# Inverting the softmax row sums of paired attention heads by two 32x32 block turns around a short reciprocal

## The chip, the cores and the metric

The kernel runs on one core of a Trainium2 chip. The metric is device time in microseconds (us). One core has a matrix engine (PE), which loads weights (PEld) and runs matmuls into PSUM; a vector engine (DVE); a scalar engine with activation functions (ACT); a general engine (POOL); and SyncE (SP), which here issues the DMAs. Each engine works through its own list of instructions in a fixed order, and engines wait for each other through semaphores.

## The reference, cut to what matters

The program is a transformer block with three branches (forgetting attention, a diagonal state-space branch called S5, attention to a memory), followed by two layers of a second kind (grouped-query attention, dilated attention, a feed-forward part). Sequence length is 512, model width 1024, and everything is float32. What the change touches is the division by the softmax sum:

```
s = q k^T (+ bias, mask);  p = softmax(s);  out = p v
```

which the kernel computes as `out = (exp(s - m) v) * (1 / sum(exp(s - m)))`. It is done for the 12 heads of the forgetting attention, and in each of the two layers for 8 heads of the grouped-query and 4 heads of the dilated attention.

## The kernel before, in words

All matmuls that feed a result of full precision are done in three passes. A float32 operand is split into a high part (`wh`, `h`, `ph`) and a low part (`wl`, `l`, `pl`). For weights, `split` casts the strip `wr`, which a DMA brought, to `wh` on ACT (L93), and subtracts on DVE or, for every few strips, on POOL (L96) to get `wl`. For activations `hsplit` does the same with ACT (L229) and DVE (L237). `pmm` is the PSUM tile of a projection; its three passes are L124 (`wh` by `h`), L125 (`wh` by `l`) and L126 (`wl` by `h`).

Attention is written as a `unit` of heads. For each head and each key block, L327 computes scores into PSUM (`ps`), ACT takes the exponential `pe` (L395) and casts it to `ph` (L397), DVE subtracts to `pl` (L399), and three matmuls (L416 to L418) add the block into `ppv`. The value operand is widened by 64 columns of ones, so that 64 of the 128 rows of `ppv` hold the head's output and the other 64 rows all hold the same row of 512 softmax sums. There is one `ppv` buffer in PSUM: the next head cannot start before this one is copied out.

`out_item(j)` does that after the head's last matmul. Two ACT copies take the sums to half of the rows of `rs` (L443) and the outputs to half of the rows of `y` (L444; in the first block it is called `yf`). After each second head of a pair, L446 inverts `rs` as a whole (128x512) on DVE and POOL multiplies (L447). There are 18 pairs: six in the first block, and in each layer four of the grouped-query attention and two of the dilated one. In the text, the six pairs of a layer are called pair 1 to pair 6, in the order of time.

What sets the order in which an engine works is neither written out by hand nor in a table:

```
with tile.TileContext(nc, schedule_with_timeline_sim=True) as tc:
```

The tile framework plays the program through a timeline of its own and fixes each engine's list from it, when the kernel is built. A change of what one operation is takes part in that, and can move instructions of all engines. One schedule-only dependency (no wait on the chip) keeps each weight cast behind the matmul that was written last before it:

```
ins = self.nc.scalar.copy(h[:, 0:m], r[:, c:c + m])
if self.pe is not None:
    self.tc.add_manual_dep(ins.ins, self.pe, self.AFTER, reason="weights")
eng.tensor_tensor(out=l[:, 0:m], in0=r[:, c:c + m], in1=f32(h)[:, 0:m], op=ALU.subtract)
```

Tiles of 128x512 come from one ring of 73 buffers (`self.u`).

Of the kernel before, what the change touches and what calls it, by code (L numbers as in the profile page):

```python
# [9 lines left out]
F32 = mybir.dt.float32  # L10
# [231 lines left out]
class Att(Core):  # L242
# [44 lines left out]
    def rows(self, mc, tag, psum_tag, out=None):  # L287
# [7 lines left out]
            nc.scalar.copy(out[96:128], pt[96:128])  # L295
        return out

    def unit(self, nh, sregs, tregs, qk, vsl, dst, extra=None, nq=4, hd=64, orow=None, fold=None):


# [3 lines left out]
        nc = self.nc  # L304
# [99 lines left out]
        def pv_item(j, i):  # L404
            ph, pl, pvs = st.pop(("p", j, i))
            pv = st["pv", j]
            mm = nc.tensor.matmul
            for x, (g, kb, c) in enumerate(pvs):
                vh, vl = vsl(j, g, kb)
                o = c  # L410
                f = i == 0 and x == 0
                z = i == nt - 1 and x == len(pvs) - 1
                if not isinstance(c, slice):
                    o = slice(0, 4 * (c[1] - c[0]))
                h, lo = self.like(ph[:, o], c), self.like(pl[:, o], c)
                mm(self.cut(pv, c), vh, h, start=f, stop=False)  # L416
                mm(self.cut(pv, c), vl, h, start=False, stop=False)  # L417
                mm(self.cut(pv, c), vh, lo, start=False, stop=z)  # L418
            if i == nt - 1:
                out_item(j)  # L420

        def vrow(j):

            if own_sum:
                return slice(0, 128)
            o = 64 * (j % 2) if orow is None else orow(j)
            return slice(o, o + 64)

        def out_item(j):
            pv = st.pop(("pv", j))  # L430
            v = vrow(j)
            if own_sum:
                rb = self.u(name="rb")
                pb = self.p("m")
                nc.tensor.matmul(pb, self.selr1[j], st["mr"], start=True, stop=True)
                nc.scalar.copy(rb, pb)
                nc.vector.tensor_tensor(out=dst(j), in0=pv, in1=rb, op=ALU.mult)
                return
            if j % 2 == 0:
                st["rs"] = self.u(name="rs")  # L440
            rows = slice(64 * (j % 2), 64 * (j % 2) + 64)
            rs, y = st["rs"], dst(j)
            nc.scalar.copy(rs[rows], pv[64 - v.start:128 - v.start])  # L443
            nc.scalar.copy(y[rows], pv[v])  # L444
            if j % 2 == 1:
                nc.vector.reciprocal(out=rs, in_=rs)  # L446
                nc.gpsimd.tensor_tensor(out=y, in0=y, in1=rs, op=ALU.mult)  # L447

        s = [(lambda j=j, q=q: s_item(j, q)) for j in range(nh) for q in range(nq)]
# [1671 lines left out]
```

## Time and profile before

| | before |
|---|---|
| median of 3 runs (lowest, highest) | 2417.26 us (2416.67, 2422.07) |
| the profiled execution: its time | 2420.52 us |
| its span in the profile | 2418.5 us |
| mean granted TensorE clock | 0.984 |
| PE busy, share of the span | 2310.7 us, 96% |
| DVE busy | 1508.5 us, 62% |
| ACT busy | 1055.8 us, 44% |
| POOL busy | 875.4 us, 36% |

Busy time counts an engine's instructions, and the end of a matmul is modelled, so PE at 96% still has gaps. About 2 us of the execution's time lie outside its span.

### The profile page before, as it was taken

What the parts mean: (1) busy time and instruction counts of PE and PEld (TensorE: products, weight loads), DVE (VectorE), ACT (ScalarE), POOL (GpSimd) and SP (SyncE); (2) the same over time, 40 slices, a digit from 0 to 9 for tenths busy, and PEclk for the clock granted to TensorE, in tenths of its full rate; (3) what the DMA queues carried; (4) which work ended last, traced back from release to release, by engine and by line L of the source; (5) the groups of instructions that cost most, each with busy time, mean ns of one, the idle gap of its engine ahead of it and who ended that gap; (6) DMA issues with size and microseconds to landing.
All of it is one profiled execution on the core that took longest, in us unless ns stands there. A gap on an engine that the chain in (4) does not pass through costs nothing.

```text
span 2418.5 us, 32948 instructions
## 1 busy us (share of the span) xinstructions
PE 2310.7 (96%) x12071; PEld 1933.5 (80%) x12098; DVE 1508.5 (62%) x2467; ACT 1055.8 (44%) x1973; POOL 875.4 (36%) x722
## 2 busy tenths in 40 slices
PE   6999999998999899999999999999899999999999
PEld 5877777877788877788888888888778888888888
DVE  6666778666899788657378673257864746422222
ACT  4354553453333436653444324334565433523432
POOL 2443556733232284235132223126521713222212
PEclk9999999999999999999999999999999999999999
DMA  5211122313576331122247563242211314223322
GB/s 171 78 44 53 44 84 95 118 49 115 207 258 247 117 107 52 53 83 85 68 132 260 199 219 122 79 140 75 79 44 51 116 53 140 75 94 111 100 84 87
DMA packets 105617, 265.37 MB, mean 110 GB/s; under 512 B 13664, under 2 KB 23408, under 8 KB 105456
## 3 DMA queue, kind: packets, MB, share of 16 engines
q1 hardware_dynamic: 104304, 261.50, 32.2%
q8 instruction: 95, 1.56, 0.3%
q10 hardware_dynamic: 1152, 1.77, 0.2%
q14 instruction: 66, 0.54, 0.1%
HBM read 244.72 MB, written 9.44 MB: 105 GB/s over the span
## 4 chain that ended last, share of the span: by engine, by line
PE 75%; DVE 11%; issue 5%; POOL 4%; ACT 3%; DMA 2%; SPq 0%; ACTq 0%; another core or an unknown queue 0%; POOLq 0%; DVEq 0%
PE pmm L124 19%; PE pmm L126 19%; PE pmm L125 19%; PE ps L327 5%; PE ppv L416 1%; PE ppv L418 1%; PE pmm L141 1%; PE ppv L417 1%; PE pmm L142 1%; PE pmm L140 1%; DVE wl L96 1%; DVE l L239 1%; ACT wh L93 1%; POOL wl L96 1%; DVE adacc L521 1%
## 5 line engine op out<-in xcount | busy, mean ns | idle before, releaser
L96 POOL TENSOR_TENSOR wl<-wr,wh 128x512 fp32r<-128x512 f32 x346 | 489.6, 1434 | 1160.3 <-ACT wh L93 1037.2
L126 PE MATMUL pmm<-h,wl 128*128 128x512 f32 (+1 forms) x2104 | 823.4, 392 | 9.0 <-POOL wl L96 5.3
L124 PE MATMUL pmm<-h,wh 128*128 128x512 f32 (+1 forms) x2104 | 823.3, 392 | 7.2 <-ACT wh L93 4.3
L125 PE MATMUL pmm<-l,wh 128*128 128x512 f32 (+1 forms) x2104 | 819.7, 390 | 0.0
L126 PEld LDWEIGHTS pmm<-h,wl 128*128 128x128 f32 x2104 | 399.6, 190 | 94.3 <-POOL wl L96 7.7
L124 PEld LDWEIGHTS pmm<-h,wh 128*128 128x128 f32 x2104 | 399.8, 190 | 86.2 <-ACT wh L93 5.6
L125 PEld LDWEIGHTS pmm<-l,wh 128*128 128x128 f32 x2104 | 399.6, 190 | 78.4 <-DVE l L237 0.8
L93 ACT CAST wh<-wr 128x512 fp32r<-128x512 f32 (+1 forms) x692 | 387.5, 612 | 146.3 <-DMA wr<-in_w 85.9
L96 DVE TENSOR_TENSOR wl<-wr,wh 128x512 fp32r<-128x512 f32 x346 | 276.2, 827 | 39.3 <-ACT wh L93 34.6
L399 DVE TENSOR_TENSOR pl<-pe,ph 128x512 fp32r<-128x512 f32 (+4 forms) x168 | 113.6, 689 | 132.1 <-ACT ph L397 131.1
L237 DVE TENSOR_TENSOR l<-r,h 128x512 fp32r<-128x512 f32 x64 | 46.6, 728 | 221.3 <-ACT h L229 216.5
L1010 DVE SCALAR_TENSOR_TENSOR x<-pmm,ada,x 128x512 f32<-128x512 f32 (+1 forms) x88 | 60.0, 682 | 178.7 <-PE pmm L126 178.3
L521 DVE SCALAR_TENSOR_TENSOR adacc<-adw,cact,adacc 128x512 f32<-128x512 f32 x168 | 154.4, 921 | 4.1 <-DMA adw<-in_wada 0.9
L327 PE MATMUL ps<-qk,qk 128*128 128x512 f32 (+4 forms) x416 | 140.8, 366 | 12.6 <-DVE unm L352 8.6
L1033 ACT ACTIVATE r<-pmm 128x512 f32<-128x512 f32 x62 | 37.1, 598 | 246.0 <-PE pmm L126 246.0
L395 ACT ACTIVATE pe<-ps 128x512 f32<-128x512 f32 (+4 forms) x168 | 84.5, 503 | 114.7 <-PE ps L327 113.3
L327 PEld LDWEIGHTS ps<-qk,qk 128*128 128x128 f32 x416 | 79.3, 192 | 29.4 <-DVE unm L352 12.4
L124 PE MATMUL pmm<-yh,wh 128*128 128x512 f32 (+1 forms) x244 | 90.4, 374 | 5.8 <-ACT yh L1466 3.8
L125 PE MATMUL pmm<-yl,wh 128*128 128x512 f32 (+1 forms) x244 | 90.4, 371 | 2.7 <-DVE yl L1128 2.7
L397 ACT CAST ph<-pe 128x512 fp32r<-128x512 f32 (+4 forms) x168 | 89.1, 530 | 6.5 <-ACT pe L395 0.4
L126 PE MATMUL pmm<-yh,wl 128*128 128x512 f32 (+1 forms) x244 | 89.5, 369 | 0.0
L352 DVE TENSOR_REDUCE unm<-ps 128x1 f32<-128x512 f32 (+2 forms) x112 | 65.1, 597 | 25.6 <-PE ps L327 25.3
(393 smaller groups left out, 3925.0 us busy)
## 6 DMA issues: line engine op xcount, KB each, us to landing
wr<-in_w SPq DMA_DIRECT2D x324, 512.0 KB
adw<-in_wada SPq DMA_DIRECT2D x192, 256.0 KB
xs<-xg SPq DMA_DIRECT2D x136, 64.0 KB
wr<-in_w SPq DMA_DIRECT2D x22, 384.0 KB
xd<-x SPq DMA_DIRECT2D x16, 256.0 KB
x<-xd SPq DMA_DIRECT2D x16, 256.0 KB
x<-in_x SPq DMA_DIRECT2D x16, 128.0 KB
x<-in_x SPq DMA_DIRECT2D x8, 256.0 KB
```

The costliest lines, as they stand in the source:

```text
L93: ins = self.nc.scalar.copy(h[:, 0:m], r[:, c:c + m])
L96: eng.tensor_tensor(out=l[:, 0:m], in0=r[:, c:c + m], in1=f32(h)[:, 0:m], op=ALU.subtract)
L124: mm(out, wh, ah, start=start, stop=False)
L125: mm(out, wh, al, start=False, stop=False)
L126: self.pe = mm(out, wl, ah, start=False, stop=stop).ins.name
L327: mm(outs[i] if len(r.shape) == 2 else outs[i].rearrange("p (r i) -> p r i", r=r.shape[1]), w, r, start=first and i == 0, stop=last and i ...
L352: nc.vector.tensor_reduce(out=nm, in_=pts[0], axis=AX.X, op=ALU.max, negate=True)
L395: nc.scalar.activation(out=e[:, w], in_=pt[:, w], func=AF.Exp)
L397: nc.scalar.copy(ph[:, w], e[:, w])
L399: nc.vector.tensor_tensor(out=pl[:, w], in0=e[:, w], in1=f32(ph)[:, w], op=ALU.subtract)
L521: nc.vector.scalar_tensor_tensor(out=acc, in0=w, scalar=cc, in1=acc, op0=ALU.mult, op1=ALU.add)
L1010: nc.vector.scalar_tensor_tensor(out=x[j][:, s], in0=pm[:, s], scalar=ada[:, c + j:c + j + 1], in1=x[j][:, s], op0=ALU.mult, op1=ALU.add)
```

## The change

`out_item` no longer inverts the whole of `rs`. A new function turns `rs` by 32x32 blocks into a tile `rt` (each block of 32 rows and 32 columns is transposed in its place). Since all 32 rows of a block hold the same 32 sums, column 0 of a turned block holds these sums, one in each row. The reciprocal is taken of that column of each of the 16 blocks in a row (128x16, a stride of 32), into `ri`. The second turn reads `ri` with each column repeated 32 times and writes the inverted sums over `rs`. The rest of `out_item` stays. `rt` takes one more tile of the ring, for a short time. All lines behind the new function stand ten lines further down (L443 becomes L453, and so on).

```diff
+    def inv_rows(self, rs):
+
+
+        nc = self.nc
+        rt = self.u(name="rt")
+        nc.vector.transpose(out=rt, in_=rs)
+        ri = self.t(self.base, [128, 16], F32, "ri", 2)
+        nc.vector.reciprocal(out=ri, in_=rt.rearrange("p (b c) -> p b c", c=32)[:, :, 0])
+        nc.vector.transpose(out=rs.rearrange("p (b c) -> p b c", c=32), in_=ri.unsqueeze(2).to_broadcast([128, 16, 32]))
...
             if j % 2 == 1:
-                nc.vector.reciprocal(out=rs, in_=rs)
+                self.inv_rows(rs)
                 nc.gpsimd.tensor_tensor(out=y, in0=y, in1=rs, op=ALU.mult)
```

**Pair 4 of the first layer.** This is ACT's list in the stretch at the end of the grouped-query attention: the exponentials of the last key block, the weight casts `wh` of a strip of the next projection, the splits `h` of the four pair outputs `y` for the branch projection, and the two copies of the pair's second head (`rs`, `y`). Before:

```order
L397 CAST ph_10071<-pe_10069 128x512
L93 CAST wh_10085<-wr_9823 128x512
L93 CAST wh_10089<-wr_9823 128x512
L945 ACTIVATE g_10120<-pmm_10095 128x512
L229 CAST h_10122<-y_9064 128x512
L229 CAST h_10126<-y_9441 128x512
L229 CAST h_10130<-y_9717 128x512
L443 COPY rs_9988<-ppv_9975 64x512
L444 COPY y_9989<-ppv_9975 64x512
L229 CAST h_10134<-y_9989 128x512
```

The same place after the change:

```order
L407 CAST ph_10107<-pe_10105 128x512
L453 COPY rs_10024<-ppv_10011 64x512
L454 COPY y_10025<-ppv_10011 64x512
L93 CAST wh_10125<-wr_9855 128x512
L93 CAST wh_10129<-wr_9855 128x512
L955 ACTIVATE g_10160<-pmm_10135 128x512
L229 CAST h_10162<-y_9088 128x512
L229 CAST h_10166<-y_9469 128x512
L229 CAST h_10170<-y_9749 128x512
L229 CAST h_10174<-y_10025 128x512
```

The two copies, which wait for the head's last matmul, now stand ahead of two weight casts, one gate activation and three splits, instead of behind them. On PE the same place reads, after the change, with the pair's last value matmul in the second of these rows and the branch projection behind it:

```order
L427 MATMUL ppv_10011<-ph_10107,vl_15_91 128x512
L428 MATMUL ppv_10011<-pl_10109,vh_14_90 128x512
L124 MATMUL pmm_10188<-h_10162,wh_10041 128x512
L124 MATMUL pmm_10300<-h_10162,wh_10041 128x512
L124 MATMUL pmm_10415<-h_10162,wh_10125 128x512
```

As before the change, the first matmul behind the pair's last one reads the split of pair 1 (`h_10162`); before, that split stood ahead of the copies on ACT, and now it stands behind them. The second layer has the same move.

**Pair 2 of the first layer.** ACT's list at the end of pair 2, where a strip's casts `wh` are followed by four casts of rotated queries and keys (`qk`). Before:

```order
L93 CAST wh_9487<-wr_9081 128x512
L93 CAST wh_9491<-wr_9081 128x512
L691 CAST qk_9525<-xg_8893 64x512
L691 CAST qk_9528<-xg_8893 64x512
L691 CAST qk_9534<-xg_9011 64x512
L443 COPY rs_9440<-ppv_9427 64x512
L444 COPY y_9441<-ppv_9427 64x512
```

After:

```order
L453 COPY rs_9468<-ppv_9455 64x512
L454 COPY y_9469<-ppv_9455 64x512
L93 CAST wh_9519<-wr_9105 128x512
L93 CAST wh_9523<-wr_9105 128x512
L701 CAST qk_9557<-xg_8917 64x512
L701 CAST qk_9560<-xg_8917 64x512
L701 CAST qk_9566<-xg_9035 64x512
```

And PE behind the pair's last value matmul, after the change:

```order
L428 MATMUL ppv_9455<-pl_9503,vh_14_90 128x512
L337 MATMUL ps_9655<-qk_9281,qk_9272 128x128
L124 MATMUL pmm_9685<-h_7648,wh_9519 128x512
L125 MATMUL pmm_9685<-l_7656,wh_9519 128x512
L126 MATMUL pmm_9685<-h_7648,wl_9520 128x512
```

The copies moved ahead of the strip's casts, and the projection that uses this strip (`wh_9519`, and `wl_9520`, which POOL makes) follows the pair's last matmul on PE at once; before, two of its matmuls stood ahead of that matmul.

**Pair 5 of the first layer.** DVE's list from the inversion to `qv`, the first step of a chain of small operations on which PE waits later. Before:

```order
L446 RECIPROCAL rs_10309<-rs_10309 128x512
L653 TENSOR_TENSOR xs_10488<-xs_10488,rope_7979 128x512
L96 TENSOR_TENSOR wl_10583<-wr_10460,wh_10582 128x512
L664 TENSOR_TENSOR xg_10487<-xg_10487,xs_10488 128x512
L951 SCALAR_TENSOR_TENSOR g_9850<-g_9850,pmm_10557 128x512
L96 TENSOR_TENSOR wl_10587<-wr_10460,wh_10586 128x512
L653 TENSOR_TENSOR xs_10539<-xs_10539,rope_7979 128x512
L660 TENSOR_SCALAR qv_10577<-ps_10531 128x4x2 x2
```

After:

```order
L303 STREAM_TRANSPOSE rt_10476<-rs_10349 128x512
L305 RECIPROCAL ri_10478<-rt_10476 128x16
L306 STREAM_TRANSPOSE rs_10349<-ri_10478 128x512
L96 TENSOR_TENSOR wl_10541<-wr_10186,wh_10540 128x512
L96 TENSOR_TENSOR wl_10545<-wr_10186,wh_10544 128x512
L663 TENSOR_TENSOR xs_10532<-xs_10532,rope_8003 128x512
L961 SCALAR_TENSOR_TENSOR g_9882<-g_9882,pmm_10601 128x512
L96 TENSOR_TENSOR wl_10627<-wr_10504,wh_10626 128x512
L96 TENSOR_TENSOR wl_10631<-wr_10504,wh_10630 128x512
L674 TENSOR_TENSOR xg_10531<-xg_10531,xs_10532 128x512
L663 TENSOR_TENSOR xs_10583<-xs_10583,rope_8003 128x512
L670 TENSOR_SCALAR qv_10621<-ps_10575 128x4x2 x2
```

The inversion moved ahead of two subtractions `wl` that stood before it, so that two more operations lie between it and `qv`.

## Rows read from the trace of the kernel before

**Rows 1.** The page's busy time of PE and DVE (us, share of the span, instructions), and its chain of work that ended last, by engine.

```profile
PE 2310.7 (96%) x12071; PEld 1933.5 (80%) x12098; DVE 1508.5 (62%) x2467; ACT 1055.8 (44%) x1973; POOL 875.4 (36%) x722
...
PE 75%; DVE 11%; issue 5%; POOL 4%; ACT 3%; DMA 2%; SPq 0%; ACTq 0%; another core or an unknown queue 0%; POOLq 0%; DVEq 0%
```

**Rows 2.** The groups of DVE instructions by line and shape: busy us, mean ns of one, idle time before them and what ended it. The inversion, and the DVE operations nearest to those that are new.

```profile
L446 DVE RECIPROCAL rs<-rs 128x512 f32<-128x512 f32 x18 | 60.2, 3344 | 18.7 <-ACT rs L443 18.7
...
L237 DVE TENSOR_TENSOR l<-r,h 128x512 fp32r<-128x512 f32 x64 | 46.6, 728 | 221.3 <-ACT h L229 216.5 <-issue 4.2
...
L653 DVE TENSOR_TENSOR xs<-xs,rope 128x512 f32<-128x512 f32 x34 | 32.2, 946 | 25.4 <-DMA xs<-xg 25.2
...
L1122 DVE TENSOR_SCALAR rd<-ph 128x512 f32<-128x512 f32 x12 | 7.1, 593 | 2.1 <-POOL ph L1284 1.6 <-POOL ph L1280 0.3
...
L375 DVE RECIPROCAL uri<-usm 128x16 f32<-128x16 f32 x2 | 0.5, 253 | 1.6 <-ACT jk L349 1.6
```

**Rows 3.** POOL's waits: total us, times, longest us.

```profile
POOL y L447 <- DVE rs L446: 34.1, 7, 11.3
```

**Rows 4.** The timeline of ACT at the end of pair 4 of the first layer: start us, us, engine line operation tiles, in brackets the idle time before and what ended it.

```profile
1030.90 1.14 ACT L93 CAST wh<-wr 128x512 fp32r<-128x512 f32 x2
1031.95 0.59 ACT L945 ACTIVATE g<-pmm 128x512 f32<-128x512 f32 x1
1032.44 1.64 ACT L229 CAST h<-y 128x512 fp32r<-128x512 f32 x3
1035.82 0.58 ACT L443 COPY rs<-ppv 64x512 f32<-64x512 f32 x1 [1.73 <-PE ppv L418]
1036.42 0.58 ACT L444 COPY y<-ppv 64x512 f32<-64x512 f32 x1
1041.25 0.63 ACT L229 CAST h<-y 128x512 fp32r<-128x512 f32 x1 [4.25 <-POOL y L447]
```

**Rows 5.** The timeline of PE at the same place: the pair's last value matmul, and the first matmuls of the branch projection.

```profile
1035.39 0.39 PE L418 MATMUL ppv<-pl,vh 128*128 128x512 f32 x1
...
1035.78 0.94 PE L124 MATMUL pmm<-h,wh 128*128 128x512 f32 x3
1036.56 0.39 PE L125 MATMUL pmm<-l,wh 128*128 128x512 f32 x1
```

**Rows 6.** The timeline of ACT at the same place of the second layer.

```profile
1836.15 1.65 ACT L229 CAST h<-y 128x512 fp32r<-128x512 f32 x3
1839.47 0.58 ACT L443 COPY rs<-ppv 64x512 f32<-64x512 f32 x1 [1.67 <-PE ppv L418]
```

**Rows 7.** The timeline of ACT at the end of pair 2 of the first layer.

```profile
972.21 1.14 ACT L93 CAST wh<-wr 128x512 fp32r<-128x512 f32 x2
973.26 1.90 ACT L691 CAST qk<-xg 64x512 fp32r<-64x512 f32 x3
975.18 0.58 ACT L443 COPY rs<-ppv 64x512 f32<-64x512 f32 x1
```

**Rows 8.** The timeline of PE there: two matmuls of the projection and the pair's last value matmul, and the gap that comes nine us later.

```profile
973.72 0.58 PE L124 MATMUL pmm<-h,wh 128*128 128x512 f32 x1
974.14 0.39 PE L125 MATMUL pmm<-l,wh 128*128 128x512 f32 x1
974.37 0.40 PE L418 MATMUL ppv<-pl,vh 128*128 128x512 f32 x1
...
983.63 0.50 PE L126 MATMUL pmm<-h,wl 128*128 128x512 f32 x1 [1.60 <-DVE wl L96]
```

**Rows 9.** The timeline of DVE and of POOL there.

```profile
977.84 3.33 DVE L446 RECIPROCAL rs<-rs 128x512 f32<-128x512 f32 x1
981.21 0.69 DVE L697 TENSOR_TENSOR kl<-xg,qk 64x512 fp32r<-64x512 f32 x1
981.93 2.67 DVE L96 TENSOR_TENSOR wl<-wr,wh 128x512 fp32r<-128x512 f32 x2
...
972.96 2.67 POOL L96 TENSOR_TENSOR wl<-wr,wh 128x512 fp32r<-128x512 f32 x2 [17.14 <-ACT wh L93]
```

**Rows 10.** The timeline of DVE, POOL and PE behind pair 5 of the first layer, from the inversion to the gap of PE.

```profile
1070.84 3.35 DVE L446 RECIPROCAL rs<-rs 128x512 f32<-128x512 f32 x1 [0.80 <-ACT rs L443]
1074.11 1.14 DVE L653 TENSOR_TENSOR xs<-xs,rope 128x512 f32<-128x512 f32 x1
...
1080.25 1.78 DVE L653 TENSOR_TENSOR xs<-xs,rope 128x512 f32<-128x512 f32 x1
1081.95 0.23 DVE L660 TENSOR_SCALAR qv<-ps 128x8 f32<-128x8 f32 x2
...
1082.26 3.33 POOL L662 TENSOR_TENSOR qv<-qv,mhalf 128x16 f32<-128x16 f32 x1 [0.78 <-DVE qv L660]
...
1089.84 0.40 PE L284 MATMUL ps<-c,mcq 128*128 128x128 bf16 x4 [1.84 <-DVE mcq L278]
```

**Rows 11.** The timeline behind pair 5 of the first block: ACT's copies, DVE's inversion and the subtractions behind it, and the gaps of PE.

```profile
313.31 0.58 ACT L443 COPY rs<-ppv 64x512 f32<-64x512 f32 x1 [4.82 <-PE ppv L418]
...
317.01 3.32 DVE L446 RECIPROCAL rs<-rs 128x512 f32<-128x512 f32 x1
...
320.82 0.50 PE L327 MATMUL ps<-qk,qk 128*128 128x512 f32 x1 [1.64 <-ACT pe L395]
325.98 0.61 PE L418 MATMUL ppv<-pl,vh 128*128 128x512 f32 x1 [3.03 <-DVE pl L399]
```

**Rows 12.** Stretches of ten us: busy us and instructions of PE, PEld, DVE, ACT and POOL, then the granted clock, the DMA share and GB/s.

```profile
310.00:320.00 10.00, 9.11 (x49) 7.21 (x48) 10.00 (x13) 3.54 (x6) 3.48 (x5) 1.00 0.39 131
320.00:330.00 10.00, 5.84 (x20) 3.92 (x21) 9.79 (x11) 7.60 (x17) 6.58 (x4) 0.83 0.04 9
980.00:990.00 10.00, 8.40 (x41) 6.48 (x40) 9.86 (x13) 5.53 (x10) 5.95 (x4) 1.00 0.30 103
1090.00:1100.00 10.00, 10.00 (x49) 8.38 (x47) 5.97 (x12) 3.39 (x6) 2.79 (x2) 0.83 0.18 60
```

## The prediction, made before the changed kernel was run

> **What bounds the kernel now.** I read the page first. PE is busy for 96% of the span, and the chain that ended last runs through PE for 75% and through DVE for 11% [rows 1]. So time is what PE does plus the gaps in which it waits, and DVE work counts only where a gap of PE hangs on it. Next I read the groups by line: the 18 inversions are 60.2 us of DVE, 3.34 us each [rows 2], and POOL waits 34.1 us in all for them [rows 3]. POOL has slack, so this is no price yet. What matters is what stands behind an inversion on DVE, and whether PE waits for that. The timeline gives the places. Behind pair 2 of a layer, PE has a gap of 1.60 us for a `wl` [rows 8] that stood behind the inversion on DVE [rows 9]. Behind pair 5, a gap of 1.84 us hangs on a chain that starts with `qv`, which came to its turn on DVE when the row of work behind the inversion was done [rows 10]. In the first block, pair 5 stands ahead of gaps of 1.64 and 3.03 us [rows 11]. At pair 4, PE runs on without a gap though ACT waits for the head's last matmul [rows 4, 5]: nothing that PE needs soon stands behind the copies.
>
> **The change on DVE.** One instruction of 3.34 us goes, three come. The reciprocal of 128x16 has a row: 0.25 us [rows 2]. A block turn of 128x512 in float32 has none. The nearest rows of that size are a subtraction (0.73 us), a product that competes with POOL (0.95) and a one-source operation (0.59) [rows 2]. From below I take two turns of 0.59, from above two of 0.95, and I choose 0.73, that of the largest group. A site then costs 2 x 0.73 + 0.25 = 1.71 us, and saves 1.63 (1.2 to 1.9): 29 us of DVE over 18 sites (21 to 34). Almost all of it lies beside PE. A second turn that reads repeated elements might be dearer; at 3.1 us for both turns nothing would be saved.
>
> The Trainium skill has a rule against such a change: the page "VectorE: DVE Perf Modes", section "The DRAIN you can't avoid", says that after each vector operation comes a flush of about its duration less 266 ns, and its rules for authors advise to keep the number of operations small. The rows here show no such pause, since the product at 1074.11 starts as the inversion ends (1070.84 and 3.35 us) [rows 10]. By the page, each turn would take an estimated 1.2 us with its flush and a site would save only 0.7 us; by the rows it saves 1.63, and the sum below would move by less than one us.
>
> **The change in the order.** This is the larger part. At several pairs the copies L443 and L444 now stand earlier in ACT's list. ACT works in order, so whatever follows the copies now waits for the head's last value matmul, and if PE needs it directly behind that matmul, PE stops.
>
> Pair 4 of each layer. PE is at the first matmul of the branch projection at 1035.78 [rows 5]. It reads the split of pair 1, which in the old list was made from 1032.44 on, ahead of the copies. In the new list it stands behind `rs`, `y`, two `wh` and one `g`. The copy began 0.43 us behind the start of the last matmul (1035.39 to 1035.82) [rows 4, 5]. With the three small score matmuls now ahead of it, that last matmul would start at about 1035.55, and `rs` at 1035.98. From there by the rows' own pitches: two copies at 0.60 each, two casts 1.05, `g` 0.49, and the first split 0.62 long, make 3.36 us [rows 4], so PE goes on at about 1039.3 instead of 1035.78: a new gap of **3.5 us**. The splits behind it come at 0.54 each and feed three passes each, so they keep ahead. Pair 4's own split is not late: by the copies and 1.7 us of DVE and 1.3 of POOL it is ready at about 1041, where before it was at 1041.25 [rows 4], with PE now later. The second layer has the same rows [rows 6]: 7.0 us together.
>
> Pair 2 of each layer. The strip's casts were made from 972.21, three us ahead of the copies [rows 7]; in the new list they stand behind them. Two matmuls of the projection stood ahead of the last value matmul (1.1 us from 973.72 with the score in between) [rows 8]; now this comes first, at about 973.9. `rs` starts 0.43 later, `y` 0.6 behind that, and the first `wh` ends 0.6 + 0.62 behind that, at 976.2, where PE is ready at 974.25: 1.95 us. Then POOL's `wl` begins, 1.33 us (half of 2.67) [rows 9], of which two matmuls (0.46) hide a part: 0.9 more. That is 2.85 us of new gaps. Against it, the old gap of 1.60 closes: the inversion ends sooner, and PE comes later. Net **+1.25** in each layer.
>
> Pair 5 of each layer. The copies move past two casts and two activations, but 23 matmuls of a projection whose weights are ready follow the last value matmul (23 x 0.23, the pitch from 974.14 to 974.37 [rows 8], is 5.3 us), which covers them. The chain to `qv` is shorter by 1.63 us on DVE and loses POOL's product from its middle, but two more `wl` stand in it now, and the first `xg` comes 2 us later out of ACT. At best 1.7 of the gap of 1.84 closes [rows 10], at worst none. I take **-0.8**.
>
> Pairs 1 and 6: the copies stay, or 26 matmuls cover them: 0. Pair 3: they move past one exponential and its cast, which PE reads more than 30 matmuls later: 0. A layer makes 3.5 + 1.25 - 0.8 = 3.95, both 7.9 us.
>
> First block. The copies of four of the six pairs move ahead of weight casts. At pair 5 this costs PE about 2.6 us at 313 (two copies and a cast, then a `wl`), and the gaps of 1.64 and 3.03 take it back, since they hang on a DMA for ACT and on DVE and not on PE [rows 11]; DVE gains 1.63 but waits longer for `rs`. The other pairs have terms of half a us to one us of both signs. I take 0, and 4 us to either side.
>
> The clock. In the stretch with the gaps of 1.64 and 3.03 the granted clock was 0.83, in the one before it 1.00; behind the gap of 1.84 it was 0.83 for ten us, with the gap of 1.60 it stayed at 1.00 [rows 12]. 0.83 over ten us is a third of the time at 1.2 instead of 2.4 GHz and costs about 1.7 us. New gaps of 3.5 us may bring it at pair 4 (twice 1.7), and the dip at 1090 may go (-1.7): I take +1.
>
> Sum: 7.9 + 0 + 1 = 8.9 us. Against the profiled execution's 2420.5 this makes 2429.4; that execution stands 3.3 us above the median, so on the median I say **2426 us**.
>
> **Rivals.** A measurement of this kernel can tell about 0.2% (4.8 us) from no change.
> - Faster. The inversion was what PE waited for, and the early copies cost nothing. Then the gaps behind inversions shrink by up to 1.63 each: pair 2 and pair 5 of both layers give 6.5, pairs 1 and 5 of the first block up to 3: about 2408. It decides if the stall at pair 4 isn't there. For it speaks that DVE is busy 9.86 of ten us behind pair 2 [rows 12]; against it, the order of ACT's list. Chance 0.15.
> - No change. The new gaps are there, but the gaps of the first block and of pair 5 close to their full size: 3.5 x 2 + 1.25 x 2 - 1.7 x 2 - 4 = +2, so 2419. Chance 0.25.
> - Slower as forecast, 2422 to 2431: 0.48.
> - Slower still, by the clock. Each of the four new gaps and one of the first block brings a dip of 1.7 us: 7.9 + 8.5 is +16, so 2434. The page "TensorE: Matmul & The Clock Gate" of the Trainium skill, Part 1, says that the array's clock is halved when it has idled, and comes back after sustained work; the dips in these rows agree. Chance 0.08.
> - The change does not do what it says: a turn takes 1.6 us or more, DVE saves nothing, and pair 2's old gap stays as well: 7.9 + 1.6 x 2 + 0.8 x 2, +13 and the clock: 2431 and more. No row here excludes it; the rows of that size speak against it. Chance 0.04.
>
> Slower by over 0.2% has 0.60, within 0.2% 0.25, faster 0.15. The range reaches from the lower part of "no change" to the clock's case: 2414 to 2434; if the stalls are as told, 2422 to 2431.
>
> **What would show it.** DVE busy falls by 21 to 34 us. At pair 4 of both layers PE has a gap of about 3.5 us before L124, with the releaser ACT `h`. At pair 2, gaps of about 2 us (ACT `wh`) and 0.9 (POOL `wl`) stand behind the last value matmul, and the old one at 983.63 is gone. At pair 5 the gap of `mcq` is between 0.1 and 1.8. The granted clock of the stretches behind pair 4 falls below 1.00, or not. The prediction is wrong if PE runs through pair 4 without a gap, or if turns take more than 1.2 us.

## The result, and the profile after

The changed kernel takes 2451.44 us (median of 4 runs, 2450.62 to 2456.20), the kernel before, beside it, 2419.20 us (4 runs). The ratio is 1.0139, with a 95% interval of 1.0127 to 1.0152: slower by some 33 us. Slower was forecast, but by 9 us, and 2451 lies beyond the end of the range (2434). The profiled execution took 2451.68 us, with a span of 2449.9 us and a mean granted clock of 0.976 (before: 2418.5 us and 0.984).

On VectorE the change did what it says. The page's busy times, answering to [rows 1]:

```profile
PE 2325.2 (95%) x12098; PEld 1946.3 (79%) x12098; DVE 1477.1 (60%) x2503; ACT 1054.6 (43%) x1973; POOL 867.5 (35%) x722
```

And the three new operations among the groups of DVE (busy us, mean ns of one, idle time before), answering to [rows 2]:

```profile
L303 DVE STREAM_TRANSPOSE rt<-rs 128x512 f32<-128x512 f32 x18 | 12.8, 709 | 42.8 <-ACT rs L453 42.7
L306 DVE STREAM_TRANSPOSE rs<-ri 128x512 f32<-128x512 f32 x18 | 12.7, 707 | 0.5
L305 DVE RECIPROCAL ri<-rt 128x16 f32<-128x16 f32 x18 | 4.5, 248 | 0.5
```

60.2 us of inversions became 30.0 us of turns and short reciprocals. DVE as a whole is busy for 31.4 us less, and the span is 31.4 us longer. The waits of PE by what they hang on (us in total, times, longest us) say where:

```profile
PE pmm L124 <- ACT wh L93: 14.0, 9, 4.5
PE ps L284 <- DVE mcq L278: 13.5, 5, 5.3
PE pmm L124 <- ACT h L229: 9.5, 4, 3.6
```

The same three groups stood at 5.7, 6.5 and 2.4 us before. All waits of PE together went from 102.8 to 120.4 us, 17.6 more. The rest of the longer span goes with the clock: PE's busy time for the same matmuls grew by 14.5 us (from 2310.7 in [rows 1] to 2325.2; 27 of the 12098 matmuls are missing from the record of before). If for every ten us of the span I take the part of full speed that was not granted as lost, the sum is 40.2 us before and 57.9 after. This sum also counts low clock while PE waits, and in some traces about 1 us behind the end of the span, so it is more than the clock costs.

By place, counted in weight loads begun: PE's work runs 4.2 us late at 400 us and 4.5 at 840, 20.0 at 1130, 19.0 at 1830 and 31.4 at 1960 (times of the kernel before). Over the attention of the first layer (845 to 1130 us) the waits grow by 7.7 us and the lost clock by 11.9, and over that of the second layer (1760 to 1960 us) by 6.4 and 8.5.

The timeline of PE at pair 4 of the first layer, answering to [rows 5]:

```profile
1045.35 0.40 PE L428 MATMUL ppv<-pl,vh 128*128 128x512 f32 x1
1049.31 0.96 PE L124 MATMUL pmm<-h,wh 128*128 128x512 f32 x3 [3.56 <-ACT h L229]
1051.28 0.80 PE L125 MATMUL pmm<-l,wh 128*128 128x512 f32 x1 [1.01 <-DVE l L237]
```

And that of ACT, answering to [rows 4]:

```profile
1045.78 0.58 ACT L453 COPY rs<-ppv 64x512 f32<-64x512 f32 x1 [4.33 <-PE ppv L428]
1046.38 0.58 ACT L454 COPY y<-ppv 64x512 f32<-64x512 f32 x1
1046.99 1.14 ACT L93 CAST wh<-wr 128x512 fp32r<-128x512 f32 x2
1048.15 0.60 ACT L955 ACTIVATE g<-pmm 128x512 f32<-128x512 f32 x1
1048.64 1.65 ACT L229 CAST h<-y 128x512 fp32r<-128x512 f32 x3
```

ACT idles 4.33 us in front of the copy, with the casts and splits that PE will want queued behind it; in [rows 4] it used that time for them. The stretches of ten us show what follows on the clock (columns as in [rows 12]):

```profile
1040.00:1050.00 10.00, 6.44 (x41) 4.78 (x40) 4.88 (x9) 5.56 (x11) 0.91 (x1) 1.00 0.15 52
1050.00:1060.00 10.00, 8.99 (x28) 6.88 (x26) 7.11 (x8) 5.45 (x12) 4.02 (x3) 0.66 0.31 105
1060.00:1070.00 10.00, 10.00 (x80) 8.90 (x78) 2.96 (x6) 3.51 (x8) 0.00 (x0) 1.00 0.01 2
```

0.66 over ten us is two thirds of the stretch at 1.2 GHz and the rest at 2.4.

### The profile page after: what moved, and what is told of

It reads as the page before. It is cut to its first block, busy times and chain, and to the rows that moved or that the text cites. A ratio compares the mean times of both kernels' runs of the same rounds, so it can differ in the third digit from the quotient of the medians.

```text
span 2449.9 us, 33000 instructions
## 1 busy us (share of the span) xinstructions
PE 2325.2 (95%) x12098; PEld 1946.3 (79%) x12098; DVE 1477.1 (60%) x2503; ACT 1054.6 (43%) x1973; POOL 867.5 (35%) x722
## 3 DMA queue, kind: packets, MB, share of 16 engines
q8 instruction: 95, 1.56, 0.3%
## 4 chain that ended last, share of the span: by engine, by line
PE 56%; issue 4%; DVE 4%; ACT 2%; POOL 1%; DMA 1%; SPq 0%; ACTq 0%; POOLq 0%; DVEq 0%
PE pmm L125 15%; PE pmm L126 15%; PE pmm L124 15%; PE ps L337 3%; PE ppv L426 1%; PE ppv L427 1%; PE ppv L428 1%; PE ps L661 1%; ACT wh L93 1%; DMA xs<-xg 1%; PE pmm L141 1%; PE pmm L140 1%; PE pmm L142 1%; DVE l L239 1%; DVE adacc L531 0%
## 5 line engine op out<-in xcount | busy, mean ns | idle before, releaser
L96 POOL TENSOR_TENSOR wl<-wr,wh 128x512 fp32r<-128x512 f32 x346 | 483.0, 1415 | 1236.8 <-ACT wh L93 1104.0
L96 DVE TENSOR_TENSOR wl<-wr,wh 128x512 fp32r<-128x512 f32 x346 | 279.7, 837 | 43.6 <-ACT wh L93 38.9
L362 DVE TENSOR_REDUCE unm<-ps 128x1 f32<-128x512 f32 (+2 forms) x112 | 65.2, 597 | 39.4 <-PE ps L337 39.0
```

The costliest lines, as they stand in the source:

```text
L362: nc.vector.tensor_reduce(out=nm, in_=pts[0], axis=AX.X, op=ALU.max, negate=True)
```

## The experiments

The two operations and the two sets of lists can be had in all four combinations: a kernel's lists are pinned row by row with schedule-only dependencies (like the one at the weight casts, no wait on the chip). In the pinned kernels with turns, the first turn writes back into `rs`. "Waits" is the total of PE's waits, "lost" the clock's sum as above, both of one profiled execution:

| kernel | operations, lists | median us (n) | ratio to before [95%] | span | waits | lost |
|---|---|---|---|---|---|---|
| before | | 2417 to 2422 | | 2418.5 | 102.8 | 40.2 |
| after | | 2451.44 (4) | 1.0139 [1.0127, 1.0152] | 2449.9 | 120.4 | 57.9 |
| turn_oldorder | turns, lists of before | 2417.42 (10) | 0.9997 [0.9988, 1.0007] | 2415.1 | 100.0 | 38.9 |
| recip_neworder | old inversion, lists of after | 2456.83 (4) | 1.0160 [1.0142, 1.0179] | 2458.8 | 124.4 | 68.0 |
| p4_old | turns, after but pair 4 | 2447.66 (4) | 1.0121 [1.0106, 1.0136] | 2443.9 | 119.1 | 53.3 |
| p4_new | turns, before but pair 4 | 2431.61 (5) | 1.0051 [1.0035, 1.0067] | 2429.6 | 105.7 | 46.4 |
| p5_new | turns, before but pair 5 | 2433.59 (4) | 1.0061 [1.0046, 1.0076] | 2430.1 | 108.5 | 43.9 |
| p45_new | turns, before but pairs 4, 5 | 2441.93 (4) | 1.0084 [1.0068, 1.0100] | 2434.1 | 109.6 | 46.3 |
| new_in_blk1 | turns, before but first block | 2428.03 (8) | 1.0035 [1.0024, 1.0046] | 2431.0 | 105.7 | 51.9 |
| turn_blk1_oldorder | turns in first block only, lists of before | 2417.42 (10) | 0.9993 [0.9984, 1.0002] | 2416.1 | 99.8 | 36.1 |

### The operations or the order?

```diff
-        rt = self.u(name="rt")
+        rt = rs
...
+    pin(tc, ORDERS)     # turn_oldorder: the lists of before
```

> The three new operations, with every engine's list in the order of the kernel before (each new operation stands where the reciprocal stood; the turn works in place, rs to rs, without a tile rt). Theory A, the lists cost the time: the old gaps behind inversions shrink, nothing new comes, 2405 to 2419 us against 2419 before. Theory B, the new operations themselves cost it (by what they hold up on DVE or by their ports): about 2445 to 2452, as in the changed kernel.

In recip_neworder the kernel before keeps its reciprocal, and the pinned lists are those of after, with the reciprocal where the short one stands.

> The old reciprocal of 128x512, with every engine's list in the order of the changed kernel. Theory A, the lists: 2450 or more, up to 2462, since each site has 1.6 us more of DVE on top of the new waits. Theory B, the new operations: about 2419.

Within the noise the order is all of it. With the lists of before, the turns neither cost nor gain anything that can be told (0.9997). With the lists of after, the old inversion is as slow as the change, or slower (1.0160). Both came out as theory A says. With the old lists, some 30 us less of DVE work are worth nothing that shows in the time.

turn_oldorder also shows where the gain went: PE is 8.5 us ahead of the kernel before at 380 us, since the gap of 3.03 us in [rows 11] halves to 1.50, and behind pair 5 of the layers the gap of `mcq` falls from 1.84 and 1.71 us to 0.94 and 1.04. It does not keep the lead: behind pair 2, for one, it waits 2.30 us in place of 1.60, and at the end of the span it is 3.4 us ahead.

In turn_blk1_oldorder the layers keep the old reciprocal and only the first block turns.

> All lists as before; the turns in the first block's six pairs, the reciprocal of 128x512 in the layers. With all 18 turned, PE was 8.5 us ahead at 380 us and back at even by the end. If the layers' turns gave it back: 2409 to 2412. If it is given back by the clock or by waits of other work whatever the layers do: 2416 to 2419.

At 400 us PE is 6 us ahead, at 700 us 4.0 and at the end 2.4: what the first block gains is given back by the work behind it, in part before the layers begin, and with the old reciprocal in the layers too.

### Which places?

Here the pinned lists are of one kernel but for some stretches, which are those of the other.

> The changed kernel with the turn in place; in the two stretches around pair 4 of the layers all lists are as before, elsewhere as in the changed kernel. Theory A1, a stall costs its length alone: the gaps of 3.56 and about 1 us go in both layers, 9 us less, 2442. Theory A2, a stall also brings a stretch at the lower clock that costs some 3.4 us more each (0.66 over the ten us behind it in the changed kernel): 16 us less, 2435. Theory B: no difference, 2450.

> All lists in the order of before but for the two stretches around pair 4, which have the order of the changed kernel; new operations, turn in place. Theory A1: 9 us above the run with all lists as before; A2: 16 us above it. Theory B: no difference between these two runs.

> All lists as before but for the stretch around pair 5 of both layers, which has the order of the changed kernel; new operations, turn in place. Theory from the run with pair 4 as before: the gap before the matmuls of mcq, 5.4 us there, comes without a stall at pair 4 to hide it: 4.5 us more than with the old lists in each layer, and the clock: 2426 to 2433 against 2417. Theory of the prediction: this order closes a part of the old gap: 2415 to 2417.

> All lists as before but for the first block, which has the order of the changed kernel; new operations, turn in place. By the shift of PE's work at 400 us (old lists: 8.5 us ahead of the kernel before; changed kernel: 4.2 us behind it) it should lose 12.7 us against the old lists: 2430. Rival: what is lost in the first block is taken up by later waits that hang on no PE work: 2417 to 2422.

By the medians, over turn_oldorder, pair 4 alone costs 14 us (11 in the repeat, p4_new_b below; the theories said 9 or 16), pair 5 alone 16, the first block alone 11. That makes 41 (38), more than the 34 of the whole; and taking pair 4 out of the whole gives back 4 us, less than either theory of p4_old said (9 or 16). p5_new and new_in_blk1 came out close to the first theory of each (2433.59 us for up to 2433, 2428.03 for 2430). Pair 2 and the start of the layers were not run alone. The ratios have intervals of 2 to 4 us to either side, so the sums alone would not show that the places overlap. The traces do, for pairs 4 and 5. In p4_old the waits of PE for `mcq` are longer than in the changed kernel, whose two behind pair 5 are 2.82 and 2.86 us:

```profile
1103.97 0.61 PE L284 MATMUL ps<-c,mcq 128*128 128x128 bf16 x4 [5.42 <-DVE mcq L278]
...
1912.28 0.61 PE L284 MATMUL ps<-c,mcq 128*128 128x128 bf16 x4 [5.80 <-DVE mcq L278]
```

The chain to `mcq` hangs on the transfers of `xs`, not on PE; a stall of PE at pair 4 is time in which that chain runs on. p45_new puts both into the old lists.

> The lists of the kernel before, with the stretches of pair 4 and of pair 5 of both layers in the order of the changed kernel (turns in place, as in p4_new and p5_new). If the two stretches cost apart from one another, the time is 2417 + 14 + 16 = 2447. If the stall of pair 4 hides a part of the wait for mcq of pair 5, as p4_old's longer mcq gaps (5.42 and 5.80 us against 2.82 and 2.86) let one expect, it is 2434 to 2441, with mcq gaps of about 2.8 us.

```profile
1091.26 0.61 PE L284 MATMUL ps<-c,mcq 128*128 128x128 bf16 x4 [2.71 <-DVE mcq L278]
...
1905.95 0.40 PE L284 MATMUL ps<-c,mcq 128*128 128x128 bf16 x4 [2.06 <-DVE mcq L278]
```

In p5_new these two are 5.12 and 4.92 us:

```profile
1089.54 0.61 PE L284 MATMUL ps<-c,mcq 128*128 128x128 bf16 x4 [5.12 <-DVE mcq L278]
```

Behind pair 4's stall they are 2.71 and 2.06, so that stall hides about half of each. The times agree, but at the edge of what they can tell: by the ratios the two places cost 0.51% (0.42% in the repeat) and 0.61% alone and 0.84% together, each with some 0.15% to either side, and the median, 2441.93 us, is at the upper end of what was expected.

### The clock

p4_new_fill is p4_new with 16 matmuls of 128x512 in each of the two stalls of pair 4, into the PSUM tile that the next matmul starts afresh; they have no use.

```diff
+        if self.fill is not None:
+            for _ in range(16):
+                self.nc.tensor.matmul(out, w[0][0][:, 0:128], self.fill, start=True, stop=True)
+            self.fill = None
```

> The run with the new lists around pair 4 alone (p4_new), and in its stall of each layer 16 more matmuls of 128x512 (3.6 us) into the PSUM tile that the next matmul starts afresh; they change no result. A2, the clock falls since PE idles, and what it costs is on top of the stall: the stretch behind pair 4 stays at 1.00, and the time falls by 5 to 8 us from p4_new's 2431.6, to about 2425. A1, the stall costs its length alone: 2431 to 2433, as p4_new.

It took 2430.46 us (5 runs; ratio 1.0036 [1.0014, 1.0057]), too close to p4_new to tell. Both were run again on one chip.

> The same kernel as p4_new, again. Ratio 1.005 (2430 to 2433 beside a kernel before at 2419).

> The same kernel as p4_new_fill, again. The 16 extra matmuls in each stall keep the granted clock at 1.00 behind it. If the lower clock behind the stalls costs what the windows say (46.4 against 32 us lost, some 5 to 8 of them behind the two stalls), it is 5 to 8 us below p4_new_b: 2423 to 2427. If the clock costs nothing here, it is within 2 us of p4_new_b.

2428.11 us (ratio 1.0042 [1.0029, 1.0054]) and 2428.99 us (1.0044 [1.0031, 1.0056]): the same time, the second case of what was expected. The stretch of pair 4 in p4_new_b:

```profile
1030.00:1040.00 10.00, 6.54 (x16) 4.71 (x17) 9.50 (x11) 9.21 (x19) 4.92 (x3) 0.66 0.16 52
1040.00:1050.00 10.00, 10.00 (x72) 8.75 (x71) 3.04 (x7) 1.72 (x5) 0.00 (x0) 1.00 0.14 52
```

And in p4_new_fill_b:

```profile
1030.00:1040.00 10.00, 8.99 (x41) 6.62 (x41) 7.00 (x9) 7.38 (x14) 3.33 (x3) 1.00 0.16 52
1040.00:1050.00 10.00, 10.00 (x70) 8.74 (x69) 5.53 (x9) 3.71 (x10) 1.62 (x1) 1.00 0.15 54
```

So the lower clock is a consequence of the stall: with PE kept at work it stays at 1.00, in the second layer too (1.00 for 0.66). What it costs at the place itself can be read from the pair's last value matmul to the first score matmul behind the projection. In p4_new_b:

```profile
1029.18 0.40 PE L428 MATMUL ppv<-pl,vh 128*128 128x512 f32 x1
...
1043.16 0.28 PE L401 MATMUL ps<-mr,c 128*128 128x256 bf16 x1
```

And in p4_new_fill_b, where the lines stand five further down:

```profile
1031.67 0.40 PE L433 MATMUL ppv<-pl,vh 128*128 128x512 f32 x1
...
1043.63 0.28 PE L406 MATMUL ps<-mr,c 128*128 128x256 bf16 x1
```

That is 13.98 us against 11.96. Over both layers and all four traces it is 14.0 to 14.5 us without the filling and 12.0 to 12.2 with it: a dip costs 2.0 to 2.5 us there, not the 3.4 of the sum over stretches of ten us. But the time is no better by the 4 us that the two places should give. Counted in weight loads, both filled traces lose some 1.7 us against p4_new_b between 1620 and 1830 us, and the medians, with intervals of 3 to 5 us to either side, neither show the rest nor rule it out. Over the whole span p4_new_fill_b lost 41.4 us of clock and p4_new_b 38.5, with dips in other places (0.66 in the ten us from 910, ahead of the first filled stall). What becomes of a dip's cost by the end of the run stays open. The profiled executions of one kernel, p4_new and p4_new_b, differ by 8 us in lost clock, and the medians of its two sets of runs by 3.5 us, so a few us of it can't be told apart by one profile.

As an account, the waits and PE's busy time fit: over turn_oldorder, the span grew by 34.8 us in after, where the waits grew by 20.4 and the busy time of the same 12098 matmuls by 14.4; by 15.0 in p5_new (8.5 and 6.2), 19.0 in p45_new (9.6 and 8.9), 15.9 in new_in_blk1 (5.7 and 10.1), 43.7 in recip_neworder (24.4 and 19.4). With lost clock in place of busy time the sums are off by more, 39.4 for 34.8 in after and 53.5 for 43.7 in recip_neworder. Over before, the changed kernel's 31.4 us are thus 17.6 of waits and some 14 of slower matmuls. Behind the stall of pair 4 in p4_new_b they start 0.43 us after each other, and 0.23 once the clock is back.

### What turns the lists over?

In the changed kernel the inversion has become shorter, and a tile of the ring was added. These two kernels keep one of the two each and leave the lists to the scheduler. turn_inplace:

```diff
-        rt = self.u(name="rt")
+        rt = rs
```

> The changed kernel with one edit: the first turn writes back into rs, so no tile rt is taken from the ring of 73 tiles of 128x512 that all such work shares (18 allocations fewer); the lists of the engines are left to the scheduler. Theory A2 (the extra ring tile, and not the turns' price, makes the scheduler put the lists in the new order): ACT's list comes out as in the kernel before at 15 of the 23 places at which the two lists differ, pair 4 of both layers among them (casts ahead of the copies), with some new deviations elsewhere. PE's wait for ACT h L229 stays under 4 us in all (9.5 after, 2.4 before), clock near 0.984, time 2417 to 2426. Rival B2 (the cheaper instructions on VectorE move the order whatever the tile): 2440 to 2455.

recip_ring is the kernel before with the tile:

```diff
-                nc.vector.reciprocal(out=rs, in_=rs)
+                rt = self.u(name="rt")
+                nc.vector.reciprocal(out=rt, in_=rs)
+                rs = rt
```

> The kernel before with one edit: the old reciprocal of 128x512 writes into a new tile rt of the ring, instead of back into rs; no turns; the lists are left to the scheduler. Theory A2: this alone gives the new lists (ACT's is as in the changed kernel at 15 of the 23 places, pair 4 and pair 5 of both layers among them), so PE's wait for ACT h L229 is some 9 us, and the time that of the changed kernel or a little over, 2445 to 2460. Rival B2: 2416 to 2425, as the kernel before.

turn_inplace: 2413.14 us (5 runs), ratio 0.9962 [0.9949, 0.9974], faster than either theory said. recip_ring: 2459.45 us (4 runs), 1.0154 [1.0140, 1.0168]. The ring tile is the cause, not the turns. ACT's list in recip_ring is that of the changed kernel at 17 of the 23 places at which the two first kernels differ, in turn_inplace it is that of before at 13, pair 4 among them (15 were expected of each). The timeline of ACT in turn_inplace, at pair 4 of the first layer:

```profile
1027.26 0.59 ACT L955 ACTIVATE g<-pmm 128x512 f32<-128x512 f32 x1
1027.75 1.65 ACT L229 CAST h<-y 128x512 fp32r<-128x512 f32 x3
1031.34 0.58 ACT L453 COPY rs<-ppv 64x512 f32<-64x512 f32 x1 [1.93 <-PE ppv L428]
1031.94 0.58 ACT L454 COPY y<-ppv 64x512 f32<-64x512 f32 x1
```

In recip_ring, where nothing on DVE became cheaper:

```profile
1047.89 0.58 ACT L443 COPY rs<-ppv 64x512 f32<-64x512 f32 x1 [3.95 <-PE ppv L418]
1048.49 0.58 ACT L444 COPY y<-ppv 64x512 f32<-64x512 f32 x1
1049.10 1.14 ACT L93 CAST wh<-wr 128x512 fp32r<-128x512 f32 x2
1050.26 0.60 ACT L947 ACTIVATE g<-pmm 128x512 f32<-128x512 f32 x1
1050.76 1.65 ACT L229 CAST h<-y 128x512 fp32r<-128x512 f32 x3
```

And its PE:

```profile
1051.42 1.22 PE L124 MATMUL pmm<-h,wh 128*128 128x512 f32 x3 [3.56 <-ACT h L229]
```

rt_own asks whether it is the ring, or a tile at all: `rt` gets two buffers of its own (the ring has 71 tiles to make room).

```diff
-        rt = self.u(name="rt")
+        rt = self.t(self.base, [128, T], F32, "rt", 2)
```

> The changed kernel with one edit: the tile rt of the turn comes from two buffers of its own, not from the ring, which is cut from 73 to 71 tiles to make room. The lists are left to the scheduler. If the ring tile is what turns the order over, ACT's list is again that of turn_inplace (3 rows differ, 131 from the changed kernel) and the time is 2410 to 2420, ratio 0.995 to 1.000. If turning out of place were the cause, or 71 tiles too few, 2440 to 2455.

2412.11 us (6 runs), ratio 0.9973 [0.9961, 0.9984]: it is the ring.

> The same kernel as turn_inplace, again: the first turn writes back into rs. If the gain is that of its lists, ratio 0.995 to 0.998; if the first result was chance, 0.999 to 1.001 as turn_oldorder.

2411.24 us (5 runs), 0.9965 [0.9952, 0.9979]: the gain holds, and this version beats both kernels, by some 8 us and some 40. In the profile of turn_inplace the waits of PE are 98.0 us, 4.8 below before, and the lost clock is 41.6; in that of turn_inplace_b they are 97.7 and 37.5. What closes are gaps behind inversions: the one of [rows 8] is gone in both, and the one of 3.03 us in [rows 11] is 0.64 and 1.62. PE is 5.0 and 6.6 us ahead of before at 400 us, and 7.4 and 9.2 at the end, where turn_oldorder kept 3.4.

Why one more tile of the ring moves the copies ahead is not settled. ACT's lists of before and after differ in 134 of 1973 rows. Built with a ring of 72, 71 or 70 tiles in place of 73, each of the two kernels changes ACT's list in 0, 3 and 19 rows, so a ring that is a tile or two shorter does not do it by itself.

## Why the prediction was wrong in size, point by point

- **DVE.** A turn was put at 0.73 us and measures 0.71, the short reciprocal 0.25 and 0.248; 29 us were to go, and 30.2 went at the inversions. Right, and so was that almost all of it lies beside PE. The pause behind each operation that the page "VectorE: DVE Perf Modes" of the Trainium skill tells of (section "The DRAIN you can't avoid") is not there: behind pair 5 (the rows further down) the reciprocal starts 0.75 us after the start of the first turn, which takes 0.71, and the second turn 0.28 us after the start of the reciprocal, which takes 0.25. The prediction's estimate by that rule, 0.7 us saved at a site, also gave the pause to the two turns alone: given to the old inversion of 3.34 us as well, the same estimate has a site save some 3.8 us, so the figure did not speak against the change. The same section says that a next operation that is not held starts earlier; whether that is why the pause is missing, no run here tests.
- **The order decides.** Right, and now shown by exchange of the lists. The prediction called it a consequence of the change as a whole; that it comes from the ring tile alone, it did not ask, though the front part shows the tile.
- **Pair 4: +3.5 in each layer.** The gap is 3.56 us in both layers, with the releaser named. What was missed is the wait behind it: "the splits behind it come at 0.54 each [...], so they keep ahead" is true of `h`, but DVE's `l` is one operation later, and PE waits another 1.01 and 0.72 us for it: 8.9 in place of 7.0. With the lower clock behind it, PE's work falls behind by 6.2 us at this place in each layer (from 9.8 us late at 1000 to 16.0 at 1060, and from 19.0 at 1830 to 25.2 at 1860).
- **Pair 2: +1.25 in each layer.** The timeline of PE, answering to [rows 8]:

```profile
982.23 0.33 PE L337 MATMUL ps<-qk,qk 128*128 128x128 f32 x1 [0.55 <-DVE ut L366]
983.59 0.50 PE L124 MATMUL pmm<-h,wh 128*128 128x512 f32 x1 [1.03 <-ACT wh L93]
...
984.94 0.50 PE L126 MATMUL pmm<-h,wl 128*128 128x512 f32 x1 [0.62 <-POOL wl L96]
```

The two gaps told are there, at 1.03 and 0.62 for 1.95 and 0.9, since PE stops 0.55 us ahead of them for something else. With the old gap gone (it is), the net is 0.6 us of waits in each layer.
- **Pair 5: -0.8 in each layer.** This step had the wrong sign. The gap of `mcq` grew from 1.84 to 2.82 us (1.71 to 2.86 in the second layer). The timeline, answering to [rows 10]:

```profile
1084.98 1.15 ACT L93 CAST wh<-wr 128x512 fp32r<-128x512 f32 x2
1086.15 0.69 ACT L642 ACTIVATE xg<-pmm,cols 128x512 f32<-128x512 f32 x1
...
1084.38 0.71 DVE L303 STREAM_TRANSPOSE rt<-rs 128x512 f32<-128x512 f32 x1 [4.97 <-ACT rs L453]
1085.13 0.25 DVE L305 RECIPROCAL ri<-rt 128x16 f32<-128x16 f32 x1
1085.41 0.71 DVE L306 STREAM_TRANSPOSE rs<-ri 128x512 f32<-128x512 f32 x1
1087.86 2.61 DVE L96 TENSOR_TENSOR wl<-wr,wh 128x512 fp32r<-128x512 f32 x2 [1.74 <-ACT wh L93]
1094.01 0.69 DVE L663 TENSOR_TENSOR xs<-xs,rope 128x512 f32<-128x512 f32 x1 [3.53 <-DMA xs<-xg]
...
1095.22 2.89 DVE L96 TENSOR_TENSOR wl<-wr,wh 128x512 fp32r<-128x512 f32 x2
...
1100.34 0.22 DVE L670 TENSOR_SCALAR qv<-ps 128x8 f32<-128x8 f32 x2
...
1108.19 0.43 PE L284 MATMUL ps<-c,mcq 128*128 128x128 bf16 x4 [2.82 <-DVE mcq L278]
```

The inversion is over early and buys nothing: DVE then idles 1.74 us for the casts and 3.53 us for a transfer. That transfer starts from `xg`, which on ACT stands behind copies and casts. The prediction saw that "the first `xg` comes 2 us later" and added up DVE's time all the same. The two `wl` behind the transfer take 2.89 us as they stand. p5_new prices this move, in both layers together, at 16 us by itself; in the changed kernel PE's work falls behind by 4.0 and 5.6 us from pair 4 to behind this gap, clock included.
- **The first block: 0, 4 to either side.** Behind it, at 400 us, PE is 4.2 us late against before, at the edge of the 4 us told. Against turn_oldorder, which is 8.5 us ahead there, the block's new order costs 12.7 us at that point, and 11 at the end when it stands alone (new_in_blk1). The one pair that was worked out, pair 5, came out as told: 1.56 us for `wh` and 0.62 for `wl` are new, the gap of 3.03 is gone, that of 1.64 is 2.05. The same move at other pairs was not worked out, and there the new waits for `wh` are as long:

```profile
159.23 0.57 PE L124 MATMUL pmm<-h,wh 128*128 128x512 f32 x1 [1.91 <-ACT wh L93]
197.99 0.58 PE L140 MATMUL pmm<-wh,h 128*128 128x256 f32 x1 [1.91 <-ACT wh L93]
243.69 0.50 PE L124 MATMUL pmm<-h,wh 128*128 128x512 f32 x1 [1.62 <-ACT wh L93]
```

"Terms of half a us to one us of both signs" was a guess where the lists would have told.
- **The start of the first layer** has no term at all. PE waits there 5.31 us for `mcq`, where two gaps of 1.76 and 1.34 us stood before.
- **The clock: +1.** Lost clock rose by 17.7 us, and PE's busy time for the same matmuls by 14.5, nearly as much as the waits. The dips used as the price were 0.83 over ten us, 1.7 us each; behind the 3.56 us stalls of pair 4 the stretch shows 0.66, which cost 2.0 to 2.5 us each where it could be tested. What was missed most is the number of dips, since there were more gaps than told. The rival "slower still, by the clock" had the mechanism, with a price somewhat too small on too few places, and a chance of 0.08. The filled stalls (1.00 for 0.66) agree with the rule of the page "TensorE: Matmul & The Clock Gate" of the Trainium skill, Part 1, that the clock falls when the array has idled.

The step that failed is thus the sum over the lists: the moves that were looked at had their first gaps priced about right where a stall follows at once (pair 4, pair 2), and were priced wrong or not at all where a chain through ACT, a transfer and DVE ends in a wait of PE much later, and the clock behind all of them was taken at 1 us, where PE's busy time shows 14.5 and the lost clock 17.7. The largest misses are pair 5 with -0.8 in each layer for 4.0 and 5.6 us of PE's lateness, pair 4 with 3.5 for 6.2, the start of the first layer with pair 2 with 1.25 for 5.3 (4.5 us late at 840, 9.8 at 1000), and the first block with 0 for 4.2.

## What to carry to other kernels

When a framework fixes the lists, an edit has two effects, that of the new operations and that of the new lists. Here the first could not be told from nothing and the second was 34 us: run the new operations with the old lists, and the old operations with the new lists, before either is believed. A temporary tile is no free choice: the same turn is 1.4% slower than before with it from the shared ring, and 0.3 to 0.4% faster in place or from buffers of its own. And an early finish on an engine that PE does not wait for is worth nothing until the last link of the chain to PE's next wait, a transfer or a cast, comes earlier too.

## What the runs showed of the hardware

- A block turn of 128x512 float32 takes DVE 0.71 us, as much as a subtraction of that size (0.73), and reading each element 32 times over costs nothing more (707 ns for 709). The reciprocal costs 3.34 us there and 0.25 us for 128x16.
- Filling a stall of 3.56 us of PE with matmuls kept the granted clock at 1.00 behind it, where it was 0.66 over ten us, and brought PE 2.0 to 2.5 us earlier through the place; no shorter run could be told. The clock that one execution loses differs by 8 us from that of another of the same kernel.
